# A one-tile loop body on VectorE, loads counted through TensorE, and a first tile moved in pieces of 1, 1 and 2 rows, in a kernel limited by its transfers

## Chip, cores, metric

One core of one Trainium2 chip. The metric is the device time of one execution in microseconds (us), lower is better. The highest and the lowest run are 0.03% apart in the kernel before (6 runs).

## The reference

```python
def reference(x):                      # x: 8 x 64 x 256 x 256, float32
    x_r = x.reshape(B, C, oH, 8, oW, 8)
    pooled = x_r.max(axis=(3, 5))      # maximum of each 8 x 8 window
    upsampled = np.repeat(np.repeat(pooled, 8, axis=2), 8, axis=3)
    return (x - upsampled).astype(np.float32)
```

It reads 134.2 MB, writes 134.2 MB, and does one maximum and one subtraction per element.

## The kernel before

The input is cut into 32 tiles of 4 MiB: 128 partitions by 4 rows of 2048 floats (a row is 8 image lines). Six buffers (slots) of 32 KiB per partition form a ring. SyncE issues loads, ScalarE issues stores, VectorE computes in place. A slot is loaded again when its store has landed.

```python
HEAD = [[2, 2]]            # pieces of the first tile, in rows
TAIL = [2, 1, 1]           # pieces of the last tile
SLOTS = 6
...
# SyncE: all loads, in order
for i in range(len(sizes)):
    slot = i % SLOTS
    if landed[slot]:
        nc.sync.wait_ge(stored[slot], 16 * landed[slot])
    ...                     # one dma_start per piece, increments first[k] or loaded[slot]
# ScalarE: all stores, in order
        done += 1
        nc.scalar.wait_ge(ready, done)
        nc.scalar.dma_start(...)
# VectorE
turns = nc.vector.alloc_register("turns")
nc.vector.reg_mov(turns, ROUNDS)
with nc.vector.If_eq(turns, 0):         # never taken
    for _ in range(SKIP):               # SKIP = 52
        nc.vector.sem_inc(skipped, 1)
...                                     # pieces of the first tile
with nc.vector.Fori(0, ROUNDS):         # 5 turns of 6 tiles
    for j in range(SLOTS):
        slot = (HEADS + j) % SLOTS
        pool_and_subtract(slot, 0, SIZE, loaded[slot])
```

`pool_and_subtract` waits for the load, reduces the tile to its window maxima in one instruction, and subtracts row by row; the last subtract increments `ready`.

## Time and profile before

| | before |
|---|---|
| time, median | 627.7 us (3 runs, 627.6 to 627.79) |
| span of the profiled execution | 626.0 us |
| VectorE busy | 562.6 us, 90% |
| transfers over the span | 429 GB/s, 433 in the middle |
| period of a tile in the loop | 19.37 us, of which VectorE works 17.73 |

The lines behind this are in the prediction. Two facts about the transfers matter later, and they come from the trace's records of single packets and landings (a transfer has 16 landings, 1088 for the 68 transfers of the kernel before; I read each as one engine's report that its share is done). A tile's load is 128 packets of 32 KiB, one per partition (3968 for 31 tiles), and its store likewise (3840 for 30). With the records put to engines as told under "The same by engine", an engine has 8 of a tile's load and 8 of its store, and while both queues hold work it alternates, one load packet, one store packet: of 8001 pairs of neighbouring records from 60 to 600 us, 7949 are of two queues (the 4-byte record that ends an engine's share of a transfer counts as a packet). From 60 to 600 us a 32 KiB packet takes 1213 ns, loads and stores alike, a pair of them 2.42 us, and eight pairs the 19.37 us of a tile. The head's packets are smaller: 16 KiB from a piece of 2 rows (611 ns), 8 KiB from one of 1 row (309 ns).

### The profile page before, as it was taken

How to read it: one execution, taken by the hardware profiler on the slowest of the kernel's cores; microseconds unless marked ns; L12 is line 12 of the kernel's file. 1: busy time of each engine (PE TensorE's matmuls, PEld its weight loads, DVE VectorE, ACT ScalarE, POOL GpSimd, SP SyncE). 2: the span in 40 equal slices, each digit the busy share in tenths (PEclk: the TensorE clock that was granted, in tenths of full speed). 3: DMA queues.
4: the chain of work that ended last, by engine and by line, in shares of the span. 5: the costliest groups of instructions: out<-in, count | busy, mean ns of one | idle time of the engine just before them, and what ended most of it. 6: DMA issues, size and time to landing. Idle time of an engine off the chain costs nothing. (4 is left out here: it accounts for less than half of the span.)

```text
span 626.0 us, 364 instructions
## 1 busy us (share of the span) xinstructions
DVE 562.6 (90%) x163; POOL 0.2 (0%) x4
## 2 busy tenths in 40 slices
DVE  4999999998998888988889888898888998888983
POOL 0000000000000000000000000000000000000000
DMA  8999999999999999999999999999999999999998
GB/s 369 399 436 437 436 436 436 436 433 427 429 431 436 427 431 436 436 436 436 436 436 436 436 431 429 427 433 429 431 433 436 436 436 436 436 436 436 436 429 343
DMA packets 9793, 268.45 MB, mean 429 GB/s; under 512 B 1088, under 2 KB 1088, under 8 KB 1088
## 3 DMA queue, kind: packets, MB, share of 16 engines
q1 hardware_dynamic: 4752, 134.22, 49.9%
q10 hardware_dynamic: 5040, 134.22, 49.7%
q14 instruction: 1, 0.01, 0.0%
HBM read 134.22 MB, written 134.22 MB: 429 GB/s over the span
## 5 line engine op out<-in xcount | busy, mean ns | idle before, releaser
L73 DVE TENSOR_REDUCE tops<-dat 128x128 f32<-128x8192 f32 (+2 forms) x35 | 278.3, 7953 | 48.9 <-DVEq L65 48.9
L85 DVE TENSOR_TENSOR dat<-dat,tops 128x2048 f32<-128x2048 f32 x128 | 285.0, 2286 | 5.2
L157 POOL MEMSET const-bfloat16-1.0<- 128x1 bf16 x1 | 0.1, 101 | 0.0
L157 POOL MEMSET const-uint8-127<- 128x1 uint8 x1 | 0.1, 101 | 0.0
L157 POOL MEMSET const-float32-0.0<- 128x1 f32 x1 | 0.1, 98 | 0.2 <-issue 0.2
L157 POOL MEMSET const-float32-1.0<- 128x1 f32 x1 | 0.1, 98 | 0.0
## 6 DMA issues: line engine op xcount, KB each, us to landing
dat<-in_x_dram SPq DMA_DIRECT2D x31, 4096.0 KB, 62.5
out_dram<-dat ACTq DMA_DIRECT2D x30, 4096.0 KB, 35.8
out_dram<-dat ACTq DMA_DIRECT2D x3, 2048.0 KB, 19.6
dat<-in_x_dram SPq DMA_DIRECT2D x2, 2048.0 KB, 9.6
out_dram<-dat ACTq DMA_DIRECT2D x2, 1024.0 KB, 9.3
```

What stands on the lines that cost most here:

```text
L73: nc.vector.tensor_reduce(out=maxs if R > 1 else maxs[:, 0], in_=(wins.rearrange("p r ph ow pw -> p r ow ph pw") if R > 1 else wins[:, 0]. ...
L85: sub = nc.vector.tensor_tensor(out=wins[:, r], in0=wins[:, r], in1=maxs[:, r].unsqueeze(1).unsqueeze(3).to_broadcast([P, pH, oW, pW]), op ...
L157: nc = _bacc.Bacc("TRN2", target_bir_lowering=False, num_devices=1)
```

## The change

Its intent, as I read it: a shorter VectorE program without padding (one tile as loop body, addresses from a register), for which the waits must be the same in every turn, so TensorE turns the six load semaphores into one count; and an earlier start, by a smaller first piece.

```diff
-HEAD = [[2, 2]]
+HEAD = [1, 1, 2]
-SKIP = 52
...
-    dats = [data.tile([P, SIZE * ROW], F32, name=f"dat{i}") for i in range(SLOTS)]
+    ring = data.tile([P, SLOTS * SIZE * ROW], F32, name="ring")
...
+        for k in range(len(HEAD)):
+            nc.tensor.wait_ge(first[k], 16).then_inc(filled, 1)
+        for i in range(1, len(sizes)):
+            turn = (i - 1) // SLOTS + 1
+            nc.tensor.wait_ge(loaded[slot_of(i)], 16 * turn).then_inc(filled, 1)
...
-        with nc.vector.Fori(0, ROUNDS):
-            for j in range(SLOTS):
-                slot = (HEADS + j) % SLOTS
-                pool_and_subtract(slot, 0, SIZE, loaded[slot])
+        with nc.vector.Fori(0, ROUNDS):
+            with nc.vector.Fori(0, SLOTS) as slot:
+                take(filled, 1)
+                pool_and_subtract(
+                    ring[:, bass.ds(slot * (SIZE * ROW), SIZE * ROW)],
+                    tops[:, bass.ds(slot * (SIZE * oW), SIZE * oW)],
+                    SIZE,
+                )
```

More of the change, by code (lines that the diff above doesn't have):

```diff
@@ L31 @@
     oW = W // pW
-    HEADS = len(HEAD)
     x_rows = x.rearrange("b c (oh ph) w -> (b c oh) (ph w)", ph=pH)
     out_rows = out.rearrange("b c (oh ph) w -> (b c oh) (ph w)", ph=pH)
-    sizes = [sum(h) for h in HEAD] + [SIZE] * (ROUNDS * SLOTS) + [sum(TAIL)]
+    sizes = [sum(HEAD)] + [SIZE] * (ROUNDS * SLOTS) + [sum(TAIL)]
     assert sum(sizes) * P == x_rows.shape[0] and max(sizes) == SIZE
     starts = [P * sum(sizes[:i]) for i in range(len(sizes))]
+    last = len(sizes) - 1
     data = ctx.enter_context(tc.tile_pool(name="data", bufs=1))
-    dats = [data.tile([P, SIZE * ROW], F32, name=f"dat{i}") for i in range(SLOTS)]
-    tops = [data.tile([P, SIZE * oW], F32, name=f"tops{i}") for i in range(SLOTS)]
-    pieces = sum(len(h) for h in HEAD)
-    first = [tc.alloc_semaphore(f"first{i}") for i in range(pieces)]
+    ring = data.tile([P, SLOTS * SIZE * ROW], F32, name="ring")
+    tops = data.tile([P, SLOTS * SIZE * oW], F32, name="tops")
+    first = [tc.alloc_semaphore(f"first{i}") for i in range(len(HEAD))]
     loaded = [tc.alloc_semaphore(f"loaded{i}") for i in range(SLOTS)]
@@ L47, with slot_of @@
     final = tc.alloc_semaphore("final")
+    filled = tc.alloc_semaphore("filled")
     reduced = tc.alloc_semaphore("reduced")
-    skipped = tc.alloc_semaphore("skipped")
     ready = tc.alloc_semaphore("ready")
+    def slot_of(i):
+        return (i - 1) % SLOTS
     def dram(rows, i):
@@ L55, in dram, with sbuf, top @@
         return rows[starts[i] : starts[i] + P * n].rearrange("(p r) d -> p (r d)", r=n)
+    def sbuf(i, lo, R):
+        at = (slot_of(i) * SIZE + lo) * ROW
+        return ring[:, at : at + R * ROW]
+    def top(i, lo, R):
+        at = (slot_of(i) * SIZE + lo) * oW
+        return tops[:, at : at + R * oW]
     def cuts(parts):
@@ L65, in take, with pool_and_subtract @@
         nc.vector.wait_ge(sem, n).then_inc(sem, -n)
-    def pool_and_subtract(slot, lo, R, wait):
-        part = dats[slot][:, lo * ROW : (lo + R) * ROW]
+    def pool_and_subtract(part, top, R):
         wins = part.rearrange("p (r ph ow pw) -> p r ph ow pw", r=R, ph=pH, ow=oW)
-        maxs = tops[slot][:, lo * oW : (lo + R) * oW].rearrange("p (r ow) -> p r ow", r=R)
-        if wait is not None:
-            take(wait, 16)
+        maxs = top.rearrange("p (r ow) -> p r ow", r=R)
         nc.vector.tensor_reduce(
@@ L91, in pool_and_subtract @@
         sub.then_inc(ready, 1)
-    last = len(sizes) - 1
     with tc.tile_critical(no_gpsimd_drain=True):
         landed = [0] * SLOTS
-        k = 0
         for i in range(len(sizes)):
-            slot = i % SLOTS
+            slot = slot_of(i)
             if landed[slot]:
                 nc.sync.wait_ge(stored[slot], 16 * landed[slot])
-            parts = HEAD[i] if i < HEADS else [sizes[i]]
-            for lo, R in cuts(parts):
+            for k, (lo, R) in enumerate(cuts(HEAD if i == 0 else [sizes[i]])):
                 part = slice(lo * ROW, (lo + R) * ROW)
-                nc.sync.dma_start(out=dats[slot][:, part], in_=dram(x_rows, i)[:, part]).then_inc(
-                    first[k] if i < HEADS else loaded[slot], 16
-                )
-                k += 1
-            landed[slot] += len(parts)
+                nc.sync.dma_start(out=sbuf(i, lo, R), in_=dram(x_rows, i)[:, part]).then_inc(
+                    first[k] if i == 0 else loaded[slot], 16
+                )
+                landed[slot] += 1
+        for k in range(len(HEAD)):
[3 more added lines that the diff above has]
+            nc.tensor.wait_ge(loaded[slot_of(i)], 16 * turn).then_inc(filled, 1)
         done = n_final = 0
         for i in range(len(sizes)):
-            slot = i % SLOTS
-            for lo, R in cuts(HEAD[i] if i < HEADS else TAIL if i == last else [SIZE]):
+            for lo, R in cuts(HEAD if i == 0 else TAIL if i == last else [SIZE]):
                 part = slice(lo * ROW, (lo + R) * ROW)
@@ L118 @@
                 nc.scalar.wait_ge(ready, done)
-                nc.scalar.dma_start(
-                    out=dram(out_rows, i)[:, part], in_=dats[slot][:, part]
-                ).then_inc(stored[slot] if i + SLOTS <= last else final, 16)
+                nc.scalar.dma_start(out=dram(out_rows, i)[:, part], in_=sbuf(i, lo, R)).then_inc(
+                    stored[slot_of(i)] if i + SLOTS <= last else final, 16
+                )
                 n_final += i + SLOTS > last
         nc.scalar.wait_ge(final, 16 * n_final)
-        turns = nc.vector.alloc_register("turns")
-        nc.vector.reg_mov(turns, ROUNDS)
-        with nc.vector.If_eq(turns, 0):
-            for _ in range(SKIP):
-                nc.vector.sem_inc(skipped, 1)
-        k = 0
-        for i in range(HEADS):
-            for lo, R in cuts(HEAD[i]):
-                pool_and_subtract(i, lo, R, first[k])
-                k += 1
-        with nc.vector.Fori(0, ROUNDS):
-            for j in range(SLOTS):
-                slot = (HEADS + j) % SLOTS
-                pool_and_subtract(slot, 0, SIZE, loaded[slot])
+        for lo, R in cuts(HEAD):
+            take(filled, 1)
+            pool_and_subtract(sbuf(0, lo, R), top(0, lo, R), R)
+        with nc.vector.Fori(0, ROUNDS):
+            with nc.vector.Fori(0, SLOTS) as slot:
+                take(filled, 1)
+                pool_and_subtract(
+                    ring[:, bass.ds(slot * (SIZE * ROW), SIZE * ROW)],
+                    tops[:, bass.ds(slot * (SIZE * oW), SIZE * oW)],
+                    SIZE,
+                )
+        take(filled, 1)
         for lo, R in cuts(TAIL):
-            pool_and_subtract(last % SLOTS, lo, R, loaded[last % SLOTS] if lo == 0 else None)
+            pool_and_subtract(sbuf(last, lo, R), top(last, lo, R), R)
 _INS = ['x']
```

## The prediction

> **What bounds the kernel now.** I read the page first, then the waits, then the timeline, then a table of stretches. The page of the kernel before:
>
> ```profile
> span 626.0 us, 364 instructions
> DVE  4999999998998888988889888898888998888983
> DMA  8999999999999999999999999999999999999998
> GB/s 369 399 436 437 436 436 436 436 433 427 429 431 436 427 431 436 436 436 436 436 436 436 436 431 429 427 433 429 431 433 436 436 436 436 436 436 436 436 429 343
> L73 DVE TENSOR_REDUCE tops<-dat 128x128 f32<-128x8192 f32 (+2 forms) x35 | 278.3, 7953 | 48.9 <-DVEq L65 48.9
> L85 DVE TENSOR_TENSOR dat<-dat,tops 128x2048 f32<-128x2048 f32 x128 | 285.0, 2286 | 5.2
> ```
>
> VectorE is busy 90% of the span and the transfers all of it: the DMA row stands at 9 from the second slice to the last but one, at about 433 GB/s. VectorE's only long idle time, 48.9 us, is spent waiting at line 65, its wait for a load. So it waits for the transfers, not they for it. The waits of both sides (us in total, times, longest):
>
> ```profile
> DVE tops L73 <- DVEq L65: 48.9, 26, 8.4
> SPq L105 <- DMA out_dram<-dat: 522.8, 26, 47.3
> ```
>
> The load queue waits for stores to free its six slots, VectorE waits for loads; both end in the transfer engines. The timeline of one tile late in the loop shows the period:
>
> ```profile
> 578.98 8.69 DVE L73 TENSOR_REDUCE tops<-dat 128x128 f32<-128x8192 f32 x1 [1.62 <-DVEq L65]
> 587.81 8.90 DVE L85 TENSOR_TENSOR dat<-dat,tops 128x2048 f32<-128x2048 f32 x4
> 596.74 20.31 ACTq L119 DMA_DIRECT2D out_dram<-dat  x4
> 598.35 4.42 DVE L73 TENSOR_REDUCE tops<-dat 128x64 f32<-128x4096 f32 x1 [1.64 <-DVEq L65]
> 614.39 2.29 DVE L85 TENSOR_TENSOR dat<-dat,tops 128x2048 f32<-128x2048 f32 x1
> ```
>
> From 578.98 to 598.35 is 19.37 us. A tile moves 4 MiB in and 4 MiB out, 8.39 MB; 8.39 MB / 19.37 us = 433 GB/s, the transfer rate again. VectorE needs 8.69 + 0.14 (gap) + 8.90 = 17.73 us of it and idles 1.63 us. That 1.63 us per tile is the room that the new loop has.
>
> The stretches (columns: stretch, its length, DVE busy, POOL busy, clock, DMA share, GB/s) show where the span is not at 433 GB/s:
>
> ```profile
> 0.00:2.00 2.00, 0.00 (x0) 0.20 (x4) 1.00 0.18 33
> 2.00:12.00 10.00, 3.59 (x1) 0.00 (x0) 1.00 0.98 401
> 12.00:20.00 8.00, 7.85 (x4) 0.00 (x0) 1.00 1.11 458
> 20.00:25.00 5.00, 4.85 (x3) 0.00 (x0) 1.00 0.87 324
> 60.00:600.00 540.00, 495.35 (x142) 0.00 (x0) 1.00 1.00 433
> 620.00:625.00 5.00, 0.00 (x0) 0.00 (x0) 1.00 0.71 301
> ```
>
> I turn each into time lost against 433 GB/s, length x (1 - rate/433): 1.85 us in 0 to 2 (the first packet starts at 1.9), 0.74 in 2 to 12, -0.46 in 12 to 20 and +1.26 in 20 to 25 (together 0.8 us around the first store), about 0.4 from 600 to 620, 1.5 in 620 to 625 and 1.0 after the last byte. Sum 6.3 us. All bytes at 433 GB/s: 268.4 MB / 433 = 619.9 us. 619.9 + 6.3 = 626.2 against a span of 626.0, so the account closes. The measured 627.7 is 1.7 us above the span. **The most that any change of this kind can win is some of those 6 us, 1%.**
>
> [...] The trace's five loop ends (line 137) show an add of 40 to 52 ns and a branch of 50 to 63 ns, some 0.1 us apart, under running subtracts. [...] The trace shows one instruction packet of 0.01 MB in the whole span, so the five branches of before fetched nothing inside the loop[...].
>
> **Part 1, the first tile in pieces of 1, 1 and 2 rows.** The first load of 2 MiB let VectorE start at 8.41. One of 1 MiB has 1.05 MB less to move, 1.05 MB / 433 = 2.4 us, so VectorE starts near 6.0. Its first store goes out after a one-row reduce (2.28), the gap (0.14) and one subtract (2.29): 10.7 instead of 17.5. This looks like a gain of 2.4 to 7 us, and I count it as none: the seven loads already queued keep the engines at full rate from about 2 us on (434, 418, 426 and 434 GB/s in 2 us stretches from 4 to 12), so an earlier store moves no byte that would otherwise be idle time; it only takes turns with a load. The end is fixed by the sum of bytes. What it adds: by the trace's packet records a packet of 32 KiB takes 1.213 us, one of 16 KiB 0.611, one of 8 KiB 0.309. Per engine 8 packets of 16 KiB become 16 of 8 KiB: 16 x 0.309 - 8 x 0.611 = 0.06 us for loads and the same for stores, +0.1 us. The loss of 0.8 us where stores begin can move with the first store and change by its own size: 0 +- 0.8 us.
>
> **Part 2, the one-tile loop body.** Removed: padding and static addresses. Added for each of 30 tiles: register work for the slot's addresses and a branch. Four row addresses in the ring and four in the maxima, with products and loop count, make about 12 register operations plus one compare-and-branch (estimate from the program text). At 0.1 us each, as line 137 shows, that is 1.3 us if nothing hides it. But VectorE's queue runs ahead: the loop end of before ran 2 us before its subtracts were done. Exposed are only those between the reduce and the first subtract, about 2 or 3, so 0.2 to 0.3 us a tile. Even all 1.3 us fits: 17.73 + 1.3 = 19.0 < 19.37. VectorE idles less, the period stays. On the end's path: 0.
>
> **Part 3, TensorE as a relay.** One semaphore hop more between a load's landing and the reduce, estimated at 0.1 to 0.2 us (VectorE itself needs 0.15 us from landing to reduce now). In the loop it lies in the 1.63 us slack and in a store queue that is always filled: a store takes 35.8 us from issue to landing, of which 9.7 is its own bytes at full rate. At the tail: the last store issues at 616.7 and lands 8.2 us later; alone, 1 MiB would take about 2.4 + 2.5 us (the first load landed 7.3 us after its issue with 4.8 us of bytes, so 2.5 us are fixed). So about 3.3 us of slack remain at the end, and 0.2 to 0.6 us of delay there costs nothing.
>
> **Sum:** 627.7 + 0.1 + 0 + 0 = **627.8 us**.
>
> **The rivals.** (a) The start counts: if the earlier first store brings forward the end, it would be by up to 2.4 us, 625.3. For it speaks that 20 to 25 ran at 324 GB/s; against it that the stretches just before and after are full, so at most 0.8 us is there to be won, 627.0. (b) VectorE becomes the bound: it must lose over 1.63 us per tile. [...]
>
> **Range and chances.** Run-to-run spread is 0.2 us. The uncertain terms are the start's 0.8 us either way and the relay. So **626.8 to 629.0** for 8 in 10. Faster than 2% means below 615.1, under the 619.9 us which the bytes need at the measured rate: **0.01**. Slower than 2% (over 640.3) takes rival (b): **0.03**. Within 2%: **0.96**.
>
> **What would show it.** If right: the loop's period stays 19.36 us; VectorE's idle time before each reduce falls from 1.63 to 1.0 to 1.5 us; the gap between reduce and first subtract grows from 0.14 to 0.3 to 0.5 us; the first reduce starts near 6.0 and the first store near 10.7, while the last load's landing (598.2) and the end move by under 1 us; GB/s stays at 433 from 60 to 600; instruction packets stay at 0 or 1. What would make it wrong: a period above 19.4 us with VectorE never waiting at its load wait (rival b), many instruction packets, or a GB/s row that differs in the middle slices.

Cut from it is what no trace or run of this case shows: figures and rules from elsewhere, a reading of the padding that rested on them, in rival (b) an assumed cost per tile with the 640 to 690 us that came of it, and rival (c), whose figure had no source. 627.7 of before, +0.1 for Part 1, 0 for Part 2 and 0 for Part 3 make the 627.8 us. The 0.03 for "slower than 2%" had rested on the assumed cost in rival (b).

## The result

The changed kernel takes **643.57 us** (median of 6 runs, 642.45 to 644.19) against 627.75 us of before (6 runs). The ratio is 1.0251, 95% interval 1.0237 to 1.0264: slower by 2.5%, outside the range of 626.8 to 629.0. Ratios here are the mean time of one kernel's fast runs over that of the other's in the same rounds, so not quite the ratio of the medians. Executions over 1.5% slower than the fastest of the same kernel are left out of the means.

The page of the changed kernel:

```profile
span 642.4 us, 619 instructions
DMA  9999999999999999999999999999999999999994
GB/s 367 441 416 441 424 422 433 431 437 422 420 424 437 424 416 431 414 433 424 416 422 420 428 428 414 426 422 426 424 420 424 426 420 426 424 424 412 428 418 203
L81 DVE TENSOR_REDUCE tops<-ring (+2 forms) x36 | 278.5, 7736 | 61.4 <-DVEq L75 61.4
L93 DVE TENSOR_TENSOR ring<-ring,tops (+1 forms) x128 | 285.1, 2286 | 5.3 <-DVEq L75 0.2
```

VectorE's work is the same to 0.3 us (278.5 + 285.1 against 278.3 + 285.0). Its idle time at the wait for a load rose from 48.9 to 61.4 us, where I had foretold a fall. The DMA row is as full as before, but the GB/s row has lost its 436s: the engines are busy all the time and move less. The waits:

```profile
DVE tops L81 <- DVEq L75: 61.4, 27, 5.8
SPq L110 <- DMA out_dram<-ring: 539.8, 26, 48.6
```

Both sides still wait for transfers. The new loop's own instructions (lines 140, 81 and 93: count, duration min/median/max in ns, first and last start):

```profile
L140 DVEq MOVE  x35: 36/36/44, 19.7 to 580.8; - x35
L140 DVEq ALU_OP  x30: 45/45/52, 34.7 to 600.5; - x30
L140 DVEq COMPARE_BRANCH  x30: 50/56/63, 34.8 to 600.6; - x30
L81 DVEq FUSED_REGOPS  x30: 99/99/99, 25.2 to 591.0; - x30
L93 DVEq FUSED_REGOPS  x90: 93/93/93, 34.2 to 600.3; - x90
```

Four short register operations, a move, an add and a branch per tile; none of them takes over 0.1 us. The page has no instruction queue any more: not one instruction packet in the span (before: one, at 17.3 us).

The stretches (start:end, length, DVE busy, POOL busy, clock, DMA share, GB/s):

```profile
0.00:2.00 2.00, 0.00 (x0) 0.20 (x4) 1.00 0.09 16
2.00:12.00 10.00, 6.08 (x3) 0.00 (x0) 1.00 1.02 416
12.00:20.00 8.00, 7.71 (x4) 0.00 (x0) 1.00 1.08 455
20.00:25.00 5.00, 4.10 (x2) 0.00 (x0) 1.00 1.01 426
25.00:60.00 35.00, 34.32 (x10) 0.00 (x0) 1.00 0.98 419
60.00:600.00 540.00, 483.88 (x138) 0.00 (x0) 1.00 1.00 425
600.00:620.00 20.00, 17.54 (x7) 0.00 (x0) 1.00 0.97 419
620.00:642.40 22.40, 9.22 (x5) 0.00 (x0) 1.00 0.62 263
```

I do the prediction's sum again, length x (1 - rate/433). From 0 to 25 the loss is 2.0 us (before: 3.4), so the start did gain 1.4 us. From 25 to 60 it is 1.1 (before: -0.2), which takes 1.3 of that back: by these windows the two kernels are about level at 60 us. From 60 to 600 it is **10.0 us** (before: 0). After 600 it is 0.65 + 8.8 = **9.4 us** (before: 2.9). All together 22.5 us, and 619.9 + 22.5 = 642.4, the span. So against the kernel before, 10 us are lost in a middle whose transfers run at 425 instead of 433 GB/s, and 6.5 us more at the end.

The packet records say which transfers: 32 KiB load packets average 1254 ns (before: 1217, all the excess at the very start), 13% of them over 1250 ns; 32 KiB store packets average 1216 (before: 1213). The excess over 1213 ns is 10.2 us per engine in loads (9.7 of it from 60 to 600 us) and 0.7 in stores: the 10 us of the middle. And the 16 engines drift apart. For the six loads into one slot, the 16 engines' landings of one load spread over 0.35 us at 25 us, 3.1 at 131, 4.0 at 250, 6.6 at 370, 9.6 at 491, 13.0 at 611. In the kernel before the same spread is 1.9 us at the first turn and a steady 2.4 from then on. At the end the engines finish one after the other: the DMA share is 0.82 from 628 to 632 us, then 0.55 to 636, 0.22 to 638, 0.10 to 640 and 0.02 after, which is the loss after 620.

**Where the stretched packets lie.** They cluster in time. Of the load packets after 60 us that lie between the first engine's end of a load tile and the last engine's end of the store tile that ends next, 23% take over 1250 ns; of those outside that window 5%. So I looked at when the two queues' tiles end. The timeline shows it without packet records: where VectorE has waited, its reduce starts 0.14 us after a load tile's last landing (0.37 in the changed kernel), and SyncE issues its next load 0.02 us after a store tile's last landing (in both). Before:

```profile
245.32 0.33 SPq L105 DMA_DIRECT2D dat<-in_x_dram  x1
248.22 0.34 ACTq L119 DMA_DIRECT2D out_dram<-dat  x1
249.83 8.69 DVE L73 TENSOR_REDUCE tops<-dat 128x128 f32<-128x8192 f32 x1 [1.64 <-DVEq L65]
```

The changed kernel:

```profile
247.74 0.34 ACTq L129 DMA_DIRECT2D out_dram<-ring  x1
250.14 8.69 DVE L81 TENSOR_REDUCE tops<-ring  x1 [2.44 <-DVEq L75]
252.28 0.33 SPq L110 DMA_DIRECT2D ring<-in_x_dram  x1
```

Before, the store tile has ended 4.5 us ahead of the load tile; in the changed kernel it ends 2.1 us after it. This is the **phase** that the experiments are about. To be free of the spread of the engines I take it from the landing records as the time of the eighth of a store tile's 16 landings less that of the nearest load tile's, averaged from 60 to 100 us: -2.6 us before, +2.4 us changed.

Why the phase stays: while both queues are filled, each engine takes one packet of each in turn (7949 of 8001 neighbouring records are of two queues before, 7819 of 7844 in the changed kernel), and the loads' lead over the stores, in packets, stays: counted over 100 to 560 us it is 22.4 packets of 32 KiB per engine before and 25.4 changed, and it moves by no more than 0.1 in that time. It is set in the first 60 us, by how far the loads have got when stores begin and by how many packets the first tile's stores have, not by their bytes (a_head1111 below moves the same bytes in 8 more of them per engine than the changed kernel, and its lead is 8.0 larger).

### The profile page after: what moved, and what is told of

It reads as the page before. It is cut to its first block, busy times and chain, and to the rows that moved or that the text cites. A ratio compares the mean times of both kernels' runs of the same rounds, so it can differ in the third digit from the quotient of the medians.

```text
span 642.4 us, 619 instructions
## 1 busy us (share of the span) xinstructions
DVE 562.8 (88%) x164; POOL 0.2 (0%) x4
## 5 line engine op out<-in xcount | busy, mean ns | idle before, releaser
L81 DVE TENSOR_REDUCE tops<-ring (+2 forms) x36 | 278.5, 7736 | 61.4 <-DVEq L75 61.4
L93 DVE TENSOR_TENSOR ring<-ring,tops (+1 forms) x128 | 285.1, 2286 | 5.3 <-DVEq L75 0.2
```

Source lines behind the costliest of these rows:

```text
L81: nc.vector.tensor_reduce(out=maxs if R > 1 else maxs[:, 0], in_=(wins.rearrange("p r ph ow pw -> p r ow ph pw") if R > 1 else wins[:, 0]. ...
L93: sub = nc.vector.tensor_tensor(out=wins[:, r], in0=wins[:, r], in1=maxs[:, r].unsqueeze(1).unsqueeze(3).to_broadcast([P, pH, oW, pW]), op ...
```

## The experiments

Eighteen runs. Theories at the outset: **V**, the loop or the relay costs the time; **H**, the head's pieces do, through the lead; **A**, address distance in memory between load and store; **P**, the engines' phase or tiles ending together.

**1. The head alone, both ways.** `a_head22`: changed kernel with

```diff
-HEAD = [1, 1, 2]
+HEAD = [2, 2]
```

> The changed kernel with the first tile again in pieces of 2 and 2 rows; the one-tile loop and the TensorE relay stay. Theory H (the head's pieces set how far the loads lead the stores, and at a lead of 4 tiles load packets stretch): the lead falls back under 4 tiles, mean 32 KiB load packet back to about 1217 ns from 1254, time 627 to 629. Theory V (loop or relay costs the time): stays at 643 to 644.

`b_head112`: kernel before with

```diff
-HEAD = [[2, 2]]
+HEAD = [[1, 1, 2]]
```

> The kernel before with only its first tile in pieces of 1, 1 and 2 rows. Theory H: becomes slow, 640 to 646, with load packets of about 1250 ns. Theory V: stays at 627 to 629.

Measured: a_head22 627.24 us (4 runs, ratio 0.9993, 0.9977 to 1.001), b_head112 643.49 us (4 runs, ratio 1.0264, 1.0245 to 1.0283). **The loop and the relay cost nothing that shows; the head alone brings the whole loss.** V falls. The page and the timeline of b_head112, with the old loop, show the changed kernel's picture, rates and phase alike:

```profile
GB/s 369 422 436 440 425 423 427 431 415 435 425 425 425 425 425 413 435 431 413 427 415 421 429 427 417 425 417 433 423 419 427 409 431 423 419 425 415 431 433 236
```

```profile
249.83 8.69 DVE L73 TENSOR_REDUCE tops<-dat 128x128 f32<-128x8192 f32 x1 [1.81 <-DVEq L65]
253.42 0.33 SPq L105 DMA_DIRECT2D dat<-in_x_dram  x1
```

**2. Addresses.** In the changed kernel load and store are 4 tiles, 16 MiB, apart for part of each tile, before never over 3 (leads of 25.4 and 22.4 packets, 8 to a tile). Both kernels were given another order of tiles, all else kept:

```diff
-        return rows[starts[i] : starts[i] + P * n].rearrange(...)
+        at = starts[ORDER[i]]
+        return rows[at : at + P * n].rearrange(...)
```

`a_apart` and `b_four` differ in the list:

> The changed kernel with its 32 tiles taken in another order, so that two tiles that are 3 or 4 turns apart are never a multiple of 4 tiles (16 MiB) apart in memory. Pieces, packet counts, queue order, slots and lead stay. Theory A (the address distance of load and store, 16 MiB or a multiple of it, stretches load packets): load packets 1213 to 1220 ns, time 627 to 629. Rival P (the 16 engines' phase, or that load and store tiles end at the same time, stretches them): stays at 642 to 645.

> The kernel before with its tiles taken in an order in which tiles 3 turns apart are 4 tiles (16 MiB) apart in memory in the first 24 turns and 12 tiles in the last 8. Its loads lead by 2 to 3 tiles, by 3 most of the time. Theory A: load packets stretch wherever the lead is 3, most of the time, so time over 645, by an estimate 650 to 670. Rival P: nothing changes, 627 to 629.

Measured: a_apart 644.29 us (ratio 1.0257), b_four 627.69 us (ratio 0.9999). The order in memory changes nothing; A falls.

**3. Lead or phase.** What is left of H is theory **L**, that loads ahead by three tiles or more are slow, and P was narrowed to theory **B**: slow when a store tile ends one packet after a load tile. `a_head13` has `HEAD = [1, 3]`, `a_head211` has `HEAD = [2, 1, 1]`; `b_late` and `a_store22`:

```diff
-                nc.scalar.wait_ge(ready, done)
+                nc.scalar.wait_ge(ready, max(done, 2))      # b_late
...
-            for lo, R in cuts(HEAD if i == 0 else ...):
-                done += 1
+            for lo, R in cuts([2, 2] if i == 0 else ...):
+                done += 1 + (done == 0)                     # a_store22
```

> The changed kernel with the first tile in pieces of 1 and 3 rows: the first store starts as early as with 1, 1, 2, but the first tile's stores are 16 packets per engine, not 24, so the loads get 8 packets (one tile) less ahead; estimate of the lead 17 packets of 32 KiB per engine against 25 (changed kernel) and 22.6 (before). Lead theory L (slow when loads lead by 24 packets, three tiles, or more): fast, 627 to 629. Boundary theory B (slow when a store tile ends one packet after a load tile, lead mod 8 of about 1): as slow as the changed kernel, 641 to 646.

> The changed kernel with the first tile in pieces of 2, 1 and 1 rows: first store as late as before and 24 packets of stores in it, so a lead of about 30.5 packets (6.5 mod 8, as before's 22.6). Theory L: the lead is at 4 tiles most of the time, slower than the changed kernel, 645 to 665. Theory B: fast, 627 to 629.

> The kernel before, pieces of 2 and 2 rows, with the first store held until the second piece is done as well (issued near 26.4 instead of 17.5). No 8 KiB packet is added; the lead rises by some 7 packets to about 30. Theory L: slow, 643 to 665. Theory B (lead 30 is 6 mod 8): 627 to 629. If it is the small packets of the head that cost: 627 to 629.

> The changed kernel, loads and VectorE's work of the first tile in 1, 1, 2 rows, but its stores in 2 and 2 rows, the first after two pieces (near 15). Lead by estimate 21 packets. Theories L and B: fast, 626.5 to 628.5. If 8 KiB load packets or the three-step start cost: 641 to 646.

Measured (2 runs each): 627.95, 627.64, 627.78 and 627.59 us. All as fast as before. Leads of 30 packets are fast, so a long lead is not what is slow (L falls, and with it H in the form that I had given it), nor are 8 KiB packets of loads or stores. My estimate for a_head13 was a miss: its lead settled at 20.2, not 17, so it did not try the phase that I meant it to try, and its result says nothing against B.

**4. Phase alone.** `a_head1111` (`HEAD = [1, 1, 1, 1]`) has a lead of just one tile more than the changed kernel, so its phase. `a_hold2` is the changed kernel with b_late's edit. `b_pause1` to `b_pause4` are the kernel before with 1, 2, 3 or 4 copies of 1024 columns by ScalarE (1045 ns each in b_pause3; two take 2.12 us in a_pause2) ahead of the first store only (here 4; `idle` is a scratch tile):

```diff
                 nc.scalar.wait_ge(ready, done)
+                for p in range(4 if done == 1 else 0):
+                    nc.scalar.copy(out=idle[:, :], in_=dats[0][:, :1024]).then_inc(paused, 1)
+                    nc.scalar.wait_ge(paused, p + 1)
```

> The changed kernel with a first tile of four single rows. The first store starts as early as in the changed kernel; 8 more store packets per engine raise the lead by exactly one tile, to about 33.5, and keep its remainder by 8 (1.5). Boundary theory B (slow when the store queue's tile ends 1 to 2 packets after the load queue's): slow, 640 to 647. If the lead of 25 itself is what is bad, or if nothing but 1, 1, 2 is: 627 to 629.

> The changed kernel, all pieces kept (loads, VectorE, stores in 1, 1, 2), only the first store held until the second piece is done too, some 4.6 us later. Lead up by about 4 packets to 29.4 (remainder 5.4, a good one so far). Theory B: fast, 627 to 629. If the number of head stores or their 8 KiB packets cost: 641 to 646.

> The kernel before with ScalarE made to copy 1024 columns four times[...] ahead of its first store only. Nothing else differs. Lead up by 3.3 to 4 packets from 22.2 to about 25.5 to 26 (remainder 1.5 to 2, the changed kernel's). Theory B: slow, 638 to 647, with landings of one transfer spread over 5 to 12 us late in the run. Otherwise 627 to 629.

> The same with two copies[...]: lead near 24, remainder 0, load and store tiles ending together. Theory B in the narrow form (1 to 2 packets): fast, 627 to 629. In the wide form (ends that coincide): slow, 635 to 647.

> The kernel before with three copies on ScalarE ahead of the first store (pause of about 3.3 us between that of two and of four copies): store tiles by estimate end 3 us after load tiles, as in the changed kernel. Boundary theory B: slowest of the pauses, 635 to 645, landing spread growing to 8 to 10 us. If only the early start of stores or the 1, 1, 2 pieces matter: 627 to 629.

> The same with one copy: store tiles end about 2 us before load tiles. If the slow range is one-sided (store end after load end): 627 to 629. If it is any meeting within 3 us: 630 to 645.

Measured: a_head1111 641.05, a_hold2 627.83, b_pause1 627.38, b_pause2 631.17 (ratio 1.0055, 1.0026 to 1.0085), b_pause4 628.21 us. b_pause3 took 673.26 us in its profiled run, which is over 1.5% above the other (both show a granted clock of 1.0), and 659.15 in its one fast run: 5% over the 627.69 of before. I had expected b_pause4 to hit the bad phase; the pauses turned out so that b_pause3 did. In its trace, which is of the slow run and so is shown for its form alone, one engine of 16 falls behind the others by over 40 us late in the run. Why b_pause3 loses twice what the other slow kernels lose stays open.

**5. Ends or issues (theory I).** The phase also sets when new transfers are issued: a load 0.02 us after a store tile's end, a store shortly before a load tile's end (in the timelines above 1.6 us ahead of the reduce before, 2.4 in the changed kernel). Three kernels move the issues and leave the ends. `a_loadlate`:

```diff
                 nc.sync.wait_ge(stored[slot], 16 * landed[slot])
+                nc.sync.wait_ge(ready, len(HEAD) + i - 3)
```

`a_storelate` and `a_storelate6` make ScalarE copy 1024 columns eight times ahead of each store `if 0 < i < last` and `if 5 < i < last`.

> The changed kernel with each load from the seventh tile on held until VectorE is done with the tile three before it, about 15 us later than now; the load queue is 57 us deep and doesn't run dry. Theory B: stays at 640 to 646. Theory I: 627 to 632.

> The changed kernel with ScalarE copying 1024 columns eight times (about 8.6 us) before each store of tiles 1 to 30; the first tile's stores and so the phase of the ends stay (+2 to +3 us). The store queue is 44.8 us deep, so it doesn't run dry. Theory B (ends meeting): stays at 641 to 646. Theory I (the store issue 3 to 5 us ahead of the load issue disturbs the packets): 627 to 632.

> The changed kernel with eight copies (8.6 us) on ScalarE before each store from tile 6 on, when the store queue is over 40 us deep. Phase stays at +2.4 us. Theory B (the ends meet one packet pair apart): slow, 640 to 646. Theory I (the time of the store issue relative to the load's end or issue): 627 to 632.

Measured: a_loadlate 642.76 us, a_storelate 627.64, a_storelate6 642.68 (4 runs, ratio 1.0236, 1.0218 to 1.0255). a_loadlate's load issue now stands next to its store issue (at 247.06 and 247.01), ahead of the load's end, and nothing is gained. a_storelate seemed to speak for the issues, but its landing records show a phase of +4.8: its fourth store was issued at 51.8 us instead of 43.1, when the third had only 1.7 us left to its landing, so the pauses had let the store queue run short and the phase moved. With them only from tile 6 on the phase stayed at +2.4 and the time stayed slow, though the store is issued 6.6 us after the reduce's start instead of 2.4 ahead:

```profile
250.85 8.69 DVE L84 TENSOR_REDUCE tops<-ring  x1 [2.09 <-DVEq L78]
254.14 0.33 SPq L113 DMA_DIRECT2D ring<-in_x_dram  x1
257.40 0.34 ACTq L136 DMA_DIRECT2D out_dram<-ring  x1
```

So the loss goes with the ends and not with the issues.

**6. The whole change, healed.** `a_pause2`: the changed kernel with two copies ahead of its first store.

```diff
                 nc.scalar.wait_ge(ready, done)
+                for _ in range(2 if done == 1 else 0):
+                    pauses += 1
+                    nc.scalar.copy(out=idle[:, :], in_=sbuf(i, 0, 1)[:, :1024]).then_inc(paused, 1)
+                    nc.scalar.wait_ge(paused, pauses)
```

> The changed kernel with two copies (about 2.3 us) on ScalarE ahead of its first store only. Loads run on meanwhile, so the lead grows by about 2 packets and the phase goes from +2.4 to about +7 us. Theory B: fast, 627 to 628.5, with 32 KiB load packets of 1213 to 1217 ns. If anything else of the change costs time: over 632.

Measured: 627.47 us (4 runs, ratio 0.9998, 0.998 to 1.0016). Its first store is issued at 12.85 instead of 10.5. **Waiting 2.3 us once at the start saves 16 us.** Page and timeline:

```profile
GB/s 369 412 441 421 436 434 436 434 436 436 432 436 436 427 423 432 436 436 434 436 434 436 436 430 436 436 432 421 432 436 436 434 436 432 436 436 432 436 436 346
```

```profile
12.85 30.34 ACTq L136 DMA_DIRECT2D out_dram<-ring  x4
...
244.21 8.69 DVE L84 TENSOR_REDUCE tops<-ring  x1 [1.64 <-DVEq L78]
251.60 0.33 SPq L113 DMA_DIRECT2D ring<-in_x_dram  x1
```

The 436s are back, VectorE's wait is 1.64 us as before, and SyncE's issue comes 7.4 us after the reduce's start.

**All runs by phase** (store tile's end after load tile's end, eighth landing, 60 to 100 us of the profiled run; one step is a packet pair, 2.42 us; for b_pause3 the time is of its fast run, the phase of its slow one):

| phase, us | steps | kernels: time, us |
|---|---|---|
| -9.7 | -4 | a_head13 628.0 (half a period, so the sign is open) |
| -7.3 | -3 | a_store22 627.6, a_hold2 627.8 |
| -4.6 to -4.8 | -2 | b_four 627.7, a_head211 627.6, b_late 627.8 |
| -2.6 | -1 | before 627.7, a_head22 627.2 |
| 0.1 | 0 | b_pause1 627.4 |
| 0.5 | 0 | b_pause2 631.2 |
| 1.9 to 2.4 | +1 | changed 643.6, b_head112 643.5, a_apart 644.3, a_loadlate 642.8, a_storelate6 642.7, a_head1111 641.1, b_pause3 659.2 |
| 4.8 | +2 | b_pause4 628.2, a_storelate 627.6 |
| 7.3 | +3 | a_pause2 627.5 |

All seven kernels with the store tile ending one packet pair after the load tile are slow, by 2.1% or more (a_head1111 and a_loadlate have two runs each, and their intervals reach down to 1.8 and 1.9%); nothing at the other steps is, save b_pause2 by 0.5%, whose engines lie on two steps. No version beats the kernel before clearly: a_head22, the best, is 0.07% faster with an interval that holds 1.

**The same by engine.** The packet records carry no engine number, but an engine's next record starts 3 or 4 ns before its last one ends, so each engine's records can be chained (from 60 to 600 us; 8001 of 8032 link before and 7844 of 7877 changed, and all but a few dozen in the others, except in b_pause3). In the changed kernel exactly one load packet lies between the record of an engine's finished load tile and that of its next finished store tile, in all 398 cases. Of the eight load packets of a tile the first three then take 1407, 1286 and 1289 ns on average and the other five 1214 to 1220. The other slow kernels show the same order, b_pause3 in 217 of 328 cases, and the same three packets. In b_pause2 a quarter of the cases (104 of 386) have that order, and only these stretch; the rest have 1213 ns throughout. No fast kernel has it, and each of the eight packets there takes 1213 to 1219 ns on average. So the condition can be read on each engine by itself.

## Why the prediction was wrong

- **What bounds the kernel**: right. Transfers before, transfers after: VectorE waits 48.9 and 61.4 us for loads, and the DMA row stands at 9 in both.
- **Part 2, the loop**: right in what it costs, too careful in its terms. The register work is 4 fused operations (93 to 99 ns) where I counted 12. The gap between reduce and first subtract, foretold to grow to 0.3 to 0.5 us, is still 0.14 us (131.90 + 8.69 to 140.73). What shows is one operation ahead of the reduce: from the end of VectorE's wait for the load to the reduce the median grew by 0.14 us. One reading was wrong: the loop end of before runs some 8.6 us ahead of the end of its last subtract (123.67 against 132.29), not 2; the error was on the careful side. Rival (b) falls: VectorE still waits 61.4 us for loads, the span has not one instruction packet, and a_head22, which keeps loop and relay, takes 627.24 us.
- **Part 3, the relay**: right. The landing records and the timeline give 0.37 us from a load tile's last landing to the reduce, 0.14 before. Of the 0.23 us more, 0.09 lie between TensorE's wait and VectorE's, which is the hop, and 0.14 are the register operation of part 2. Both are paid in idle time.
- **Part 1, the start itself**: right as far as VectorE goes. First reduce 5.77 (foretold 6.0), first store 10.5 (foretold 10.7). The dip from 20 to 25 us went away, 426 instead of 324 GB/s, and the first 25 us gained 1.4 us, though I had allowed 0.8; by 60 us 1.3 of it was gone again.
- **Part 1, the step that failed**: "it only takes turns with a load. The end is fixed by the sum of bytes." I took 433 GB/s for a property of the engines that holds in whatever order loads and stores take turns. That was my assumption; the trace of before shows the rate in one order only. That the queues take turns packet by packet seemed to say that the order cannot matter, and is what makes it matter: with it the lead that the first 60 us produce stays to within 0.1 packet. The changed head put the store tile's end one packet pair after the load tile's, and there the engines run at 425 GB/s and drift apart. That term, 0 +- 0.8 us in my sum, measured +10 us in the middle and +6.5 us at the end. The loop's period rose to 20.0 us while VectorE still waited for loads.
- **The rivals and the chances**: none of the rivals had it. I named "a GB/s row that differs in the middle slices" as a sign of being wrong, which it was. I gave 0.03 to slower by over 2%, all of it to rival (b). A profile of one kernel cannot show that its transfer rate depends on a phase that never varies in it; the honest answer to that is a wider range for a change that moves the start of a queue.

**What is shown and what is open.** Shown: the head causes the loss, by the moment of the first store (a_pause2 and a_hold2 remove it, b_pause3 brings it about with the old head), not by its packet sizes, the lead's length, addresses, or the issue times; and the loss goes with one phase. Open: why an engine's load packets stretch there. The engines' drift goes with the stretch and may come of it; which of the two drives the other no run isolates.

## What to carry to other kernels

With one load queue and one store queue both kept full, and tiles of equal size, their relative position was frozen early here (a lead of 22.4 or 25.4 packets that moved by no more than 0.1 from 100 to 560 us), and an edit of the first microseconds changed the rate of the whole middle (425 instead of 433 GB/s): compare the GB/s row of the middle, not only the start. If the engines are fully busy and the rate has fallen, look for when the two queues' tiles end relative to each other and how far the engines' landings spread; then try a different head, or several delays of 1 to 4 us ahead of the first store (one of the four tried here made a fast kernel slow), before blaming the computation. And test each part of a mixed change alone: here the two suspected parts, the loop and the relay, were innocent.
